# Attention probabilities of twelve heads turned by VectorE and a trip through device memory instead of by TensorE

## The chip, the cores and the metric

The kernel runs on one core of a Trainium2 chip. The metric is device time in microseconds for one execution. The core's engines work from separate instruction queues: TensorE (PE in the profile, its weight loads PEld), VectorE (DVE), ScalarE (ACT), GpSimd (POOL) and SyncE (SP), which here only issues transfers. An instruction that has to wait holds up whatever stands behind it in its own queue.

## The reference, cut to what matters

The program is a two-layer decoder trunk over 256 tokens of width 1024. Each layer is a half-weighted SwiGLU block of width 2816, a mixer, and a second SwiGLU block.

```python
for layer in range(2):
    h = h + 0.5 * swiglu(rms_norm(h, ffn1_norm[layer]), ...)
    hn = rms_norm(h, mix_norm[layer])
    h = h + (ab_mixer(hn, ...) if layer % 2 == 0 else c_mixer(hn, ...))
    h = h + 0.5 * swiglu(rms_norm(h, ffn2_norm[layer]), ...)
return rms_norm(h, final_norm)

def swiglu(x, w_gate, w_up, w_down):
    return (silu(x @ w_gate) * (x @ w_up)) @ w_down
```

The even layer's mixer (`ab_mixer`) has 8 attention heads of 64 with three dilated windows beside a gated position mixing; the odd layer's (`c_mixer`) has 16 heads of 64 with block-sparse attention. At 256 tokens both come down to causal softmax attention over all 256 keys, the even one with a mask that counts in how many windows a key lies. Per head this is

```python
p = softmax(q @ k.T * 64 ** -0.5 + mask)     # 256 queries x 256 keys, causal
out = p @ v
```

## The kernel before

**Numbers.** Every matrix is used as a high part (rounded to the matmul's format, float32r) and a low part (the rest). A product is three matmuls: high x high, high x low, low x high (`mm3`, L265). `split` (L270) makes both parts of a tile: ScalarE copies the high part, VectorE subtracts it for the low one.

**Weights.** They come as 171 pieces of up to 1 MB (`raw`) through SyncE's queue. `Stream` keeps three raw buffers (`RAW`) and four pairs of parts (`SPL`). `take` hands TensorE the next piece; `free` gives a piece back, and `pump` then splits the piece four ahead (L172 on ScalarE, L173 on VectorE) and issues the load three further on (L139).

**Order.** Inside the framework a planner puts each engine's instructions in a fixed order before the run, by its own estimate of when inputs are ready and by the order in which they are written. `tc.issue_after(x)` makes the instructions in its block stand behind `x` on the engine that both use. A tile's buffer is handed to the next tile of its name when everything that reads the old one is done; a transfer that reads it counts.

**Steps.** The mixers write the order of the attention work by hand. `Slots.at((5, 6, ...), f)` says at which step `f` is called; `step()` is called after every tile of matmuls, so step n comes right behind the n-th one. A step of the projections is 24 matmuls of 256 columns or 12 of 512. In the odd layer steps 0 to 3 are the first q and k tiles, 4 to 7 a block of v, 8 to 11 q and k of the second column group, 12 to 15 q and k of the third, 16 to 19 v, 20 to 23 q and k of the fourth, and 24 to 31 lie in the output projection. In the even layer 4 to 7 are v, 8 to 11 the gate's values, 12 to 19 u, q and k, and 20 to 27 the projection.

**Attention of a head.** `put_q` and `put_k` (L665, L677) make q and k with both parts from TensorE's banks; k's low half is written by GpSimd (L685) in the odd layer. `scores(h)` (L691) is four matmuls (L700, L701), then per half: VectorE adds the mask and takes the maximum (L704), ScalarE the exponential and its sum (L707), VectorE the reciprocal (L710), GpSimd (VectorE for the last heads) the multiplication (L714). The result is `pr`, 128 x 384: the first 128 queries with 128 keys, and the second 128 queries with 256. `turn(h)` (L718) transposes it on TensorE in three pieces of 128 x 128 (L723) into a bank and splits it into `pth` and `ptl` (L726). `weighted(p)` (L728) multiplies a pair of heads with v, three matmuls of 512 columns and three of 256, and splits the result into `mix`.

In the odd layer before, the heads' scores stand at steps 5 to 8, 12 to 19, 24, 24, 25 and 25; their turns at 9, 9, 11, 11, 16, 16, 18, 18, 20, 20, 22, 22, 26, 26, 27 and 27; the eight sums at 11, 13, 18, 20, 22, 24, 28 and 29. In the even layer scores stand at 6 to 9, 20, 20, 21, 21, turns at 10, 10, 12, 12, 22, 22, 23, 23, sums at 13, 14, 24, 25.

The kernel already has one trip through device memory: `turn_back` in the last SwiGLU block (L486) turns the residual in blocks of 32 x 32 on VectorE (L491, a 32 x 32 block stays in its place among the blocks), sends 512 KB to memory (`away`, L494) and fetches it with its blocks moved (`xr`, L496, four fetches of 128 KB).

Of the kernel before, what the change touches and what calls it, by code (L numbers as in the profile page):

```python
# [35 lines left out]
LINE, SHIFT = 64, 16  # L36
EDGE, GAP = 56, 240

# [76 lines left out]
class Stream:  # L115


    def __init__(self, nc, pools, weights):
        self.nc, (self.raw_pool, self.hi_pool, self.lo_pool) = nc, pools
        self.weights = weights  # L120
        self.specs, self.raws, self.parts = [], {}, {}
        self.loaded = self.split = self.done = self.next = 0
        self.held = False

    def add(self, nk, w, shift, cuts, reset):
# [4 lines left out]
    def load_one(self, between=lambda i: None):  # L130
        j = self.loaded
        nk, w, loads, *_ = self.specs[j]
        raw = self.raw_pool.tile([128, CH], F32, name="raw")
        n = nk * w // loads
        for i in range(loads):
            between(i)
            cs = slice(i * n, (i + 1) * n)
            src = self.weights[j, i * 128 * n : (i + 1) * 128 * n].rearrange("(p c) -> p c", p=128)
            self.nc.sync.dma_start(raw[:, cs], src)  # L139
        self.raws[j] = raw  # L140
        self.loaded += 1
# [5 lines left out]
    def split_parts(self):  # L147
# [19 lines left out]
        def split(a, r):  # L167
            n = r.free_size()
            hi, lo = his[:, a : a + n], los[:, a : a + n]
            if len(r.shape) == 3:  # L170
                hi, lo = (t.rearrange("p (k c) -> p k c", k=reset) for t in (hi, lo))
            nc.scalar.activation(hi, r, AF.Copy)  # L172
            nc.vector.tensor_sub(lo, r, hi.bitcast(F32))  # L173

# [50 lines left out]
def trunk(ctx: ExitStack, tc: tile.TileContext, a, out):  # L225
# [11 lines left out]
    def bank():  # L237
        return ps.tile([128, 512], F32, name="bank")
# [406 lines left out]
    def make_attention(mp, mask_cols, nheads, v, mix, rows=False):  # L645

        qs, ks, probs, pts = {}, {}, {}, {}
        pairs, flying = (4, 5) if rows else (2, 4)
        seconds = [mp.tile([128, 2 * S + LINE], F32R, name=f"ql{i}") for i in range(pairs)]
# [7 lines left out]
        def scaled(bk):  # L657
            t = mp.tile([128, S], F32, name="qk", bufs=3)
            nc.vector.tensor_mul(t, bk[:, :S], norm["row"])
            return t  # L660
# [30 lines left out]
        def scores(h):  # L691
            q, ql = qs.pop(h)
            k = ks.pop(h)
            sc = bank()
            pr = mp.tile([128, 384], F32, name="pr", bufs=flying)
            nm = wk.tile([128, 2], F32, name="nm")
# [19 lines left out]
            return power, share  # L716

        def turn(h):  # L718
            p, j = divmod(h, 2)
            pr = probs.pop(h)  # L720
            tp = bank()
            for i in range(3):
                nc.tensor.transpose(tp[:, i * 128 : (i + 1) * 128], pr[:, i * 128 : (i + 1) * 128], ident)  # L723
            if j == 0:
                pts[p] = [mp.tile([128, 2, 384], F32R, name=n, bufs=2) for n in ("pth", "ptl")]
            return split(pts[p][0][:, j, :], pts[p][1][:, j, :], tp[:, :384])  # L726

        def weighted(p):  # L728
            o = bank().rearrange("p (j c) -> p j c", j=2)
            pth, ptl = pts.pop(p)  # L730
            vs = slice(p * 128, (p + 1) * 128)
            mm3(o, v[0][:, 0, vs], v[1][:, 0, vs], pth[:, :, :256], ptl[:, :, :256], True, False)
            mm3(o[:, :, 128:], v[0][:, 1, vs], v[1][:, 1, vs], pth[:, :, 256:], ptl[:, :, 256:], False, True)
            for j in range(2):
                r = slice(j * 64, j * 64 + 64)
                done = split(mix[0][r, p], mix[1][r, p], o[r, j, :].rearrange("p (t c) -> p t c", t=NT))
            return done

        return put_q, put_k, scores, turn, weighted

# [83 lines left out]
    def ab_mixer(phase):  # L824
        with tc.tile_pool(name="mp", bufs=1) as mp:
# [3 lines left out]
            uT = mp.tile([128, 4, S], F32, name="uT")  # L829
            put_q, put_k, scores, turn, weighted = make_attention(mp, slice(0, 384), 8, v, mix)  # L830

# [63 lines left out]
    def c_mixer(phase):  # L895
        with tc.tile_pool(name="mp", bufs=1) as mp:
            mix = mix_tiles(mp)
            v = v_tiles(mp, D)
            put_q, put_k, scores, turn, weighted = make_attention(mp, slice(384, 768), 16, v, mix, True)
# [90 lines left out]
```

## Time and profile before

| what | value |
|---|---|
| median of three runs | 937.8 us (937.56 to 938.14) |
| the profiled execution | 937.0 us |
| its span, first to last instruction | 935.3 us |
| granted TensorE clock | 0.999 |
| TensorE busy | 927.7 us, 99% |
| VectorE, ScalarE, GpSimd busy | 612.1, 499.2, 83.0 us |
| even layer's attention in the span | about 206 to 269 us |
| odd layer's attention in the span | about 655 to 740 us |

Busy time of TensorE is modelled: a matmul's length in the profile includes its pipeline, and the next one starts long before the last one ends. What an instruction costs the stream is the distance from its start to the next start. For the other engines the length is the cost, apart from small overlaps. A timeline row has start, length, engine, line, operation and tiles, then how many were merged. A row of the groups has after the bar the busy time in all, the mean in ns, and the idle time before it.

### The profile page before, as it was taken

The numbers are of one execution on the slowest core, as the hardware profiler recorded it, in microseconds if no ns is written. First come the engines' busy times: TensorE is split into PE (matmuls) and PEld (weight loads), VectorE is DVE, ScalarE is ACT, GpSimd is POOL, SyncE is SP. The second block draws the span as 40 slices with busy tenths as digits, with TensorE's granted clock in tenths as the row PEclk, the third lists the DMA queues.
The fourth block names the chain that finished last, engine by engine and source line by source line (L and its number), as shares of the span: only waits on it lengthen the run. The fifth ranks groups of instructions, "written<-read, shape, count | busy, mean of one in ns | idle before, by whom it ended". The sixth has DMA issues, their size and how long they took to land.

```text
span 935.3 us, 18101 instructions
## 1 busy us (share of the span) xinstructions
PE 927.7 (99%) x7655; PEld 907.4 (97%) x7655; DVE 612.1 (65%) x892; ACT 499.2 (53%) x782; POOL 83.0 (9%) x114
## 2 busy tenths in 40 slices
PE   9999999999999999999999999999999999999997
PEld 9999999999999999999999999999999999999886
DVE  7866556676888666555756665567787786656543
ACT  7744444468667454444454544456786665445431
POOL 0000000034210000000000000002574000000000
PEclk9999999999999999999999999999999999999999
DMA  8755554665336555555555555556543377555521
GB/s 320 281 212 181 189 194 162 223 222 180 136 136 226 188 211 188 183 175 206 204 184 200 204 180 170 203 184 220 177 139 136 137 243 269 186 188 210 190 90 46
DMA packets 28305, 176.99 MB, mean 189 GB/s; under 512 B 3264, under 2 KB 4672, under 8 KB 9152
## 3 DMA queue, kind: packets, MB, share of 16 engines
q1 hardware_dynamic: 26928, 173.65, 52.5%
q10 hardware_dynamic: 1296, 2.18, 0.7%
q8 instruction: 60, 0.98, 0.4%
q14 instruction: 21, 0.17, 0.0%
HBM read 173.72 MB, written 2.10 MB: 188 GB/s over the span
## 4 chain that ended last, share of the span: by engine, by line
PE 98%; issue 1%; DMA 0%; ACT 0%; SPq 0%; DVE 0%; POOLq 0%; POOL 0%
PE bank L266 30%; PE bank L267 30%; PE bank L268 30%; PE bank L567 2%; PE bank L571 2%; PE bank L568 2%; PE bank L723 1%; PE bank L700 1%; PE bank L701 1%; DMA x<-in_x 0%; PE bank L343 0%; PE bank L859 0%; PE bank L361 0%; PE bank L455 0%; PE bank L456 0%
## 5 line engine op out<-in xcount | busy, mean ns | idle before, releaser
L172 ACT ACTIVATE whi<-raw 128x1024 fp32r<-128x1024 f32 (+3 forms) x352 | 330.5, 985 | 350.1 <-issue 282.9
L173 DVE TENSOR_TENSOR wlo<-raw,whi 128x1024 fp32r<-128x1024 f32 (+3 forms) x352 | 389.6, 1141 | 126.7 <-ACT whi L172 125.8
L266 PE MATMUL bank<-xTh,whi 128*128 128x256 f32 x1616 | 447.9, 277 | 0.0
L267 PE MATMUL bank<-xTl,whi 128*128 128x256 f32 x1616 | 446.7, 276 | 0.0
L268 PE MATMUL bank<-xTh,wlo 128*128 128x256 f32 x1616 | 446.6, 276 | 0.0
L267 PEld LDWEIGHTS bank<-xTl,whi 128*128 128x128 f32 x1616 | 303.5, 188 | 0.2
L266 PEld LDWEIGHTS bank<-xTh,whi 128*128 128x128 f32 x1616 | 303.5, 188 | 0.0
L268 PEld LDWEIGHTS bank<-xTh,wlo 128*128 128x128 f32 x1616 | 303.5, 188 | 0.0
L267 PE MATMUL bank<-hTl,whi 128*128 128x256 f32 x528 | 145.8, 276 | 0.0
L266 PE MATMUL bank<-hTh,whi 128*128 128x256 f32 x528 | 145.8, 276 | 0.0
L268 PE MATMUL bank<-hTh,wlo 128*128 128x256 f32 x528 | 145.8, 276 | 0.0
L266 PEld LDWEIGHTS bank<-hTh,whi 128*128 128x128 f32 x528 | 99.1, 188 | 0.0
L268 PEld LDWEIGHTS bank<-hTh,wlo 128*128 128x128 f32 x528 | 99.1, 188 | 0.0
L267 PEld LDWEIGHTS bank<-hTl,whi 128*128 128x128 f32 x528 | 99.1, 188 | 0.0
L506 DVE TENSOR_TENSOR hm<-gs,bank 128x512 f32<-128x512 f32 x44 | 30.1, 687 | 77.7 <-PE bank L268 77.3
L503 DVE TENSOR_TENSOR gs<-bank,row 128x512 f32<-128x512 f32 x44 | 30.0, 689 | 47.8 <-PE bank L268 47.8
L266 PE MATMUL bank<-mixh,whi 128*128 128x256 f32 x128 | 35.3, 281 | 0.0
L267 PE MATMUL bank<-mixl,whi 128*128 128x256 f32 x128 | 35.1, 277 | 0.0
L268 PE MATMUL bank<-mixh,wlo 128*128 128x256 f32 x128 | 35.0, 277 | 0.0
L714 POOL TENSOR_SCALAR pr<-pr,rl 128x128 f32<-128x128 f32 (+1 forms) x36 | 30.8, 870 | 25.2 <-DVE rl L710 14.1
L653 POOL MEMSET ql<- 64x256 f32 x12 | 3.7, 307 | 328.7 <-ACT whi L172 170.3
L567 PE MATMUL bank<-whi,hTh 128*128 128x512 f32 x80 | 31.1, 389 | 0.0
(134 smaller groups left out, 877.4 us busy)
## 6 DMA issues: line engine op xcount, KB each, us to landing
raw<-in_weights SPq DMA_DIRECT2D x149, 1024.0 KB, 4.9
raw<-in_weights SPq DMA_DIRECT2D x12, 768.0 KB, 4.4
raw<-in_weights SPq DMA_DIRECT2D x6, 512.0 KB, 6.5
x<-in_x SPq DMA_DIRECT2D x4, 264.0 KB, 4.0
raw<-in_weights SPq DMA_DIRECT2D x4, 256.0 KB, 4.3
away<-xn SPq DMA_DIRECT2D x2, 512.0 KB, 5.5
xr<-away SPq DMA_DIRECT2D x8, 128.0 KB, 5.7
fg<-in_final_norm ACTq DMA_DIRECT2D x1, 512.0 KB, 3.7
```

The costliest lines, as they stand in the source:

```text
L172: nc.scalar.activation(hi, r, AF.Copy)
L173: nc.vector.tensor_sub(lo, r, hi.bitcast(F32))
L266: nc.tensor.matmul(p, sh, mh, start=start, stop=False)
L267: nc.tensor.matmul(p, sh, ml, start=False, stop=False)
L268: nc.tensor.matmul(p, sl, mh, start=False, stop=stop)
L503: nc.vector.tensor_mul(g, both(pg), twice(norm["row"]))
L506: nc.vector.tensor_mul(hm, g, both(pu))
L567: nc.tensor.matmul(banks[t, h], sh, w[0][kw][:, cs], start=k == 0, stop=False)
L568: nc.tensor.matmul(banks[t, h], sh, w[1][kw][:, cs], start=False, stop=False)
L571: nc.tensor.matmul(banks[t, h], sl, w[0][kw][:, cs], start=False, stop=k == FT - 1)
L700: nc.tensor.matmul(sc[:, b * S : (b + 1) * S], q[:, bs], k, start=True, stop=False)
L714: share = engine.tensor_scalar(pr[:, cs], pr[:, cs], rl[:, b : b + 1], None, op0=ALU.mult)
```

## The change

Heads 0 to 3 of the even layer and 0 to 7 of the odd layer, in groups of four, no longer go through `turn`. Instead, two steps behind the scores (three for head 3 of the even layer), `tilt(h)` transposes the 32 x 32 blocks of `pr` in place among the blocks on VectorE, into a tile `turned` that holds four heads. `send(g)` writes this tile to device memory in four transfers, in pieces of 512 bytes; `fetch(g)` brings it back in four transfers with the blocks moved, in pieces of 2 KB, into what will be `ptl`. Both go through SyncE's queue, the fetch right behind the send, and the next weight load behind the fetch (`st.turn`). Five steps later `part(g)` makes the high part on ScalarE and the low part in place on VectorE, in two halves each, behind the last split of weights that was written before it. The other twelve heads are turned on TensorE as before.

`pth` and `ptl` now hold four heads, a block of 32 queries at a time with the four heads beside each other, and have one buffer where pairs had two; `weighted` and its split read and write that order. `pr` has three buffers where it had five (odd) and four (even); the scores of the later heads go into `turned` and, in the odd layer, partly into `pr`. `qk` has two buffers where it had three, and an unused gap tile before the activations shrinks from 240 to 112 words. Scores, turns and sums of the odd layer move to other steps.

```diff
-EDGE, GAP = 56, 240
+EDGE, GAP = 56, 112
@@ Stream.load_one
-            self.nc.sync.dma_start(raw[:, cs], src)
+            with self.turn.pop()() if self.turn else ExitStack():
+                self.nc.sync.dma_start(raw[:, cs], src)
@@ Stream.split_parts
-            nc.scalar.activation(hi, r, AF.Copy)
-            nc.vector.tensor_sub(lo, r, hi.bitcast(F32))
+            self.last = nc.scalar.activation(hi, r, AF.Copy), nc.vector.tensor_sub(lo, r, hi.bitcast(F32))
@@ make_attention
-        pairs, flying = (4, 5) if rows else (2, 4)
+        pairs = 4 if rows else 2
+        late = nheads // 2
...
-            t = mp.tile([128, S], F32, name="qk", bufs=3)
+            t = mp.tile([128, S], F32, name="qk", bufs=2)
@@ scores
-            pr = mp.tile([128, 384], F32, name="pr", bufs=flying)
+            if h < late or rows and 12 <= h < 15:
+                pr = mp.tile([128, 384], F32, name="pr", bufs=3)
+            else:
+                if h % 4 == 0 or h == 15:
+                    probs["turned"] = turned_tile()
+                pr = probs["turned"].rearrange("p m j h r -> p (m j h r)")[:, h % 4 * 384 : (h % 4 + 1) * 384]
...
-            nc.vector.reciprocal(rl, l)
+            probs["behind"] = nc.vector.reciprocal(rl, l)
@@ new
+        def turned_tile():
+            return mp.tile([128, 3, 4, 4, 32], F32, name="turned")
+
+        def tilt(h):
+            if h % 4 == 0:
+                probs["turned"] = turned_tile()
+            turned = probs["turned"]
+            behind = st.last[1] if h % 4 == 3 else probs["behind"]
+            with tc.issue_after(behind.ins):
+                nc.vector.transpose(turned[:, :, :, h % 4].rearrange("p m j r -> p (m j) r"),
+                                    probs.pop(h).rearrange("p (b c) -> p b c", c=32))
+
+        def send(g):
+            sent[g] = dram.tile([32, 12, 4, 128], F32, name=f"sent{nheads}{g}")
+            for i in range(4):
+                nc.sync.dma_start(sent[g][:, :, i],
+                                  probs["turned"][i * 32 : (i + 1) * 32].rearrange("c m j h r -> c (m j) (h r)"))
+
+        def fetch(g):
+            src = sent.pop(g).rearrange("c (m j) i f -> j c m (i f)", j=4)
+            pts[g] = parts = part_tiles()
+            for j in range(4):
+                back = nc.sync.dma_start(parts[1][j * 32 : (j + 1) * 32].bitcast(F32).rearrange("p (m i) h r -> p m (i h r)", m=3),
+                                         src[j])
+            st.turn.append(lambda: tc.issue_after(back.ins))
+
+        def part(g):
+            with tc.issue_after(st.last[0].ins), tc.issue_after(st.last[1].ins):
+                for q in range(2):
+                    hi, lo = (t[:, q * 6 : (q + 1) * 6] for t in pts[g])
+                    nc.scalar.activation(hi, lo.bitcast(F32), AF.Copy)
+                    nc.vector.tensor_sub(lo, lo.bitcast(F32), hi.bitcast(F32))
+
+        def part_tiles():
+            return [mp.tile([128, 12, 4, 32], F32R, name=n) for n in ("pth", "ptl")]
@@ turn
-                pts[p] = [mp.tile([128, 2, 384], F32R, name=n, bufs=2) for n in ("pth", "ptl")]
-            return split(pts[p][0][:, j, :], pts[p][1][:, j, :], tp[:, :384])
+                pts[g] = part_tiles()
+            return split(*(t[:, :, j] for t in pts[g]), tp[:, :384].rearrange("p (b r) -> p b r", r=32))
@@ weighted
-            mm3(o, v[0][:, 0, vs], v[1][:, 0, vs], pth[:, :, :256], ptl[:, :, :256], True, False)
-            mm3(o[:, :, 128:], v[0][:, 1, vs], v[1][:, 1, vs], pth[:, :, 256:], ptl[:, :, 256:], False, True)
+            for b, (q, n) in enumerate(((slice(0, 8), 0), (slice(8, 12), 256))):
+                mm3(o[:, n:], v[0][:, b, vs], v[1][:, b, vs],
+                    *(t[:, q, hs].rearrange("p b h r -> p b (h r)") for t in pts[p // 2]), b == 0, b == 1)
@@ ab_mixer
-            slots.at((10, 10, 12, 12, 22), turn)
+            slots.at((8, 9, 10, 12), tilt)
+            slots.at((12,), send)
+            slots.at((12,), fetch)
+            slots.at((17,), part)
+            slots.at((22,), lambda _: turn(4))
...
-            slots.at((13, 14, 24), weighted)
+            slots.at((18, 19, 24), weighted)
@@ c_mixer
-            slots.at((5, 6, 7, 8, 12, 13, 14, 15, 16, 17, 18, 19, 24, 24, 25, 25), scores)
-            slots.at((9, 9, 11, 11, 16, 16, 18, 18, 20, 20, 22, 22, 26, 26, 27, 27), turn)
-            slots.at((11, 13, 18, 20, 22, 24, 28, 29), weighted)
+            slots.at((5, 6, 7, 8, 11, 12, 13, 14, 17, 18, 19, 20, 23, 24, 25, 25), scores)
+            slots.at((7, 8, 9, 10, 13, 14, 15, 16), tilt)
+            slots.at((10, 16), send)
+            slots.at((10, 16), fetch)
+            slots.at((15, 21), part)
+            slots.at((16, 17, 22, 22, 25, 26, 28, 29), weighted)
+            slots.at((23, 23, 24, 24, 26, 26, 27, 27), lambda i: turn(8 + i))
```

More of the change, by code (lines that the diff above doesn't have):

```diff
@@ L123, in __init__ @@
         self.held = False
+        self.turn = []
     def add(self, nk, w, shift, cuts, reset):
@@ L724, in turn @@
             if j == 0:
-                pts[p] = [mp.tile([128, 2, 384], F32R, name=n, bufs=2) for n in ("pth", "ptl")]
-            return split(pts[p][0][:, j, :], pts[p][1][:, j, :], tp[:, :384])
+                pts[g] = part_tiles()
+            return split(*(t[:, :, j] for t in pts[g]), tp[:, :384].rearrange("p (b r) -> p b r", r=32))
         def weighted(p):
-            o = bank().rearrange("p (j c) -> p j c", j=2)
-            pth, ptl = pts.pop(p)
+            o = bank()
+            hs = slice(p % 2 * 2, p % 2 * 2 + 2)
             vs = slice(p * 128, (p + 1) * 128)
-            mm3(o, v[0][:, 0, vs], v[1][:, 0, vs], pth[:, :, :256], ptl[:, :, :256], True, False)
-            mm3(o[:, :, 128:], v[0][:, 1, vs], v[1][:, 1, vs], pth[:, :, 256:], ptl[:, :, 256:], False, True)
+            for b, (q, n) in enumerate(((slice(0, 8), 0), (slice(8, 12), 256))):
+                mm3(o[:, n:], v[0][:, b, vs], v[1][:, b, vs],
+                    *(t[:, q, hs].rearrange("p b h r -> p b (h r)") for t in pts[p // 2]), b == 0, b == 1)
             for j in range(2):
                 r = slice(j * 64, j * 64 + 64)
-                done = split(mix[0][r, p], mix[1][r, p], o[r, j, :].rearrange("p (t c) -> p t c", t=NT))
+                done = split(*(m[r, p].rearrange("p t (i r) -> p (t i) r", r=32) for m in mix),
+                             o[r].rearrange("p (b h r) -> p b h r", h=2, r=32)[:, :, j])
             return done
-        return put_q, put_k, scores, turn, weighted
+        return put_q, put_k, scores, tilt, send, fetch, part, turn, weighted
     def mix_tiles(mp):
@@ L829, in ab_mixer @@
             uT = mp.tile([128, 4, S], F32, name="uT")
-            put_q, put_k, scores, turn, weighted = make_attention(mp, slice(0, 384), 8, v, mix)
+            put_q, put_k, scores, tilt, send, fetch, part, turn, weighted = make_attention(mp, slice(0, 384), 8, v, mix)
             vgain = mp.tile([128, 512], F32, name="vgain")
```

6 lines of the change are left out of this document (3 added, 3 removed).

## The prediction

> **What bounds the kernel now.** I read the page's engine shares and its chain first, to see which engine sets the end.
>
> ```profile
> span 935.3 us, 18101 instructions
> ...
> PE 927.7 (99%) x7655; PEld 907.4 (97%) x7655; DVE 612.1 (65%) x892; ACT 499.2 (53%) x782; POOL 83.0 (9%) x114
> ...
> PE 98%; issue 1%; DMA 0%; ACT 0%; SPq 0%; DVE 0%; POOLq 0%; POOL 0%
> ...
> L723 PE MATMUL bank<-ident,pr 128*128 128x128 f32 x72 | 9.9, 273 | 0.0
> ```
>
> TensorE is busy from end to end and the chain is its own stream. So time taken out of that stream shortens the run one for one, and every wait put into it lengthens it one for one. The last row, from the groups by line, is what the change halves: 72 transposes, three for each of 24 heads. Its 273 ns is the length of one with its pipeline, not what it costs the stream. For that I read TensorE's timeline, where the cost is the distance between starts.
>
> ```profile
> 216.92 0.40 PE L266 MATMUL bank<-whi,xTh 128*128 128x512 f32 x1
> ...
> 219.68 0.82 PE L723 MATMUL bank<-ident,pr 128*128 128x128 f32 x6
> ...
> 223.09 0.28 PE L266 MATMUL bank<-xTh,whi 128*128 128x256 f32 x1
> ...
> 225.84 0.82 PE L723 MATMUL bank<-ident,pr 128*128 128x128 f32 x6
> ...
> 244.00 0.37 PE L266 MATMUL bank<-xTh,whi 128*128 128x256 f32 x1
> ...
> 665.38 0.28 PE L700 MATMUL bank<-k,q 128*128 128x256 f32 x1
> ...
> 665.84 0.28 PE L266 MATMUL bank<-xTh,whi 128*128 128x256 f32 x1
> ...
> 668.56 0.82 PE L723 MATMUL bank<-ident,pr 128*128 128x128 f32 x6
> ...
> 674.68 0.82 PE L723 MATMUL bank<-ident,pr 128*128 128x128 f32 x6
> ...
> 682.73 0.40 PE L266 MATMUL bank<-pth,vth 128*128 128x512 f32 x1
> ...
> 683.78 0.28 PE L266 MATMUL bank<-xTh,whi 128*128 128x256 f32 x1
> ...
> 690.14 0.40 PE L266 MATMUL bank<-whi,xTh 128*128 128x512 f32 x1
> ...
> 734.21 0.90 PE L723 MATMUL bank<-ident,pr 128*128 128x128 f32 x6
> ```
>
> From 216.92 to 219.68 run the twelve matmuls of one step of a token block, 2.76 us. From 219.68 to 223.09 run six transposes (two heads) and the same twelve again, 3.41 us: the six cost 0.65. In the odd layer one step of 24 small matmuls takes 2.72 us (665.84 to 668.56); six transposes and two such steps take 6.12 (668.56 to 674.68), which leaves 0.68. The stages also give the other steps: scores of a head 0.46 us (665.38 to 665.84), a weighted sum of a pair 1.05 (682.73 to 683.78).
>
> **What leaves TensorE.** Twelve heads (0 to 3 of the even layer, 0 to 7 of the odd one) lose their turns: six groups at 0.65 to 0.68 us, **4.0 us** off the path. Nothing is added to TensorE: scores and weighted sums keep their number. But all twelve pairs' sums now read the probabilities in runs of 64 words (eight or four runs a matmul), where before each matmul read two runs. Before, three matmuls at 512 and three at 256, with six gaps, take 1.05 us; the same sizes without a gap would be 3 x 2.76 / 12 + 3 x 2.72 / 24 = 1.03. I take zero; six gaps at 0.02 us make thirty gaps 0.10, which is 0.08 more a pair and bounds it at 1.0 us in all. The moved addresses (the smaller gap tile, the larger turned tile) I also take at zero: the three lines of the main matmuls read different tiles, and the page gives them 277, 276 and 276 ns.
>
> **What VectorE and ScalarE get.** These rows are from the groups by line with shapes apart.
>
> ```profile
> L173 DVE TENSOR_TENSOR wlo<-raw,whi 128x768 fp32r<-128x768 f32 x26 | 23.8, 954 | 26.1 <-ACT whi L172 25.8
> ...
> L173 DVE TENSOR_TENSOR wlo<-raw,whi 128x384 fp32r<-128x384 f32 x32 | 17.5, 576 | 5.0 <-ACT whi L172 5.0
> ...
> L271 DVE TENSOR_TENSOR ptl<-bank,pth 128x384 fp32r<-128x384 f32 x24 | 12.3, 547 | 2.1 <-ACT pth L271 2.0
> ...
> L491 DVE STREAM_TRANSPOSE xn<-x 128x128 f32<-128x128 f32 x16 | 3.6, 278 | 0.0
> ...
> L172 ACT ACTIVATE whi<-raw 128x768 fp32r<-128x768 f32 x26 | 20.7, 839 | 39.6 <-issue 39.6
> ...
> L271 ACT ACTIVATE pth<-bank 128x384 fp32r<-128x384 f32 x24 | 10.5, 486 | 0.5 <-PE bank L723 0.2
> ```
>
> For four heads VectorE loses four low parts at 547 ns (2.19 us) and gains four tilts and two low parts over 768 columns at 954 ns (1.91). A tilt of 384 columns lies between 576 ns (the plain operation of that width) and three times 278 (834); I take 0.58. That is +2.0 us a group, at most +3.1. ScalarE goes from four at 486 to two at 839, 0.3 less. Neither engine is the bound; what hides the extra is the lead of the weights' halves.
>
> ```profile
> 671.42 1.00 DVE L271 TENSOR_TENSOR ptl<-bank,pth 128x384 fp32r<-128x384 f32 x2
> ...
> 672.91 1.23 DVE L173 TENSOR_TENSOR wlo<-raw,whi 128x1024 fp32r<-128x1024 f32 x1
> 674.17 0.42 DVE L659 TENSOR_TENSOR qk<-bank,row 128x256 f32<-128x256 f32 x1
> ...
> 674.20 0.33 SPq L139 DMA_DIRECT2D raw<-in_weights  x1
> ...
> 690.49 1.05 ACT L172 ACTIVATE whi<-raw 128x1024 fp32r<-128x1024 f32 x1
> ...
> 675.13 1.54 POOL L685 TENSOR_TENSOR k<-qk,k 64x256 fp32r<-64x256 f32 x2 [2.46 <-ACT k L683]
> ...
> 225.92 1.49 DVE L173 TENSOR_TENSOR wlo<-raw,whi 128x1280 fp32r<-128x1280 f32 x1 [0.55 <-ACT whi L172]
> ...
> 690.00:710.00 20.00, 20.00 (x122) 17.74 (x121) 16.37 (x43) 16.64 (x43) 13.69 (x16) 1.00 0.38 138
> ```
>
> (Timelines of several engines, and last a stretch: VectorE is its fourth busy time, 16.37 of 20 us.) The chunk whose low half ends at 674.14 is four chunks ahead of TensorE, which takes it at 690.14: **16 us of cover** for VectorE and ScalarE. The load issued at 674.20 feeds the third split after it, at 690.49: also 16 us, of which a landing takes about 5. If that cover were gone, every late half would stall TensorE in full.
>
> **The queue of SyncE.** Each group adds four sends and four fetches of 197 KB to the queue that issues the weights. The fetches wait in it for the sends, and the next weight load stands behind them. The nearest rows are the existing trip through memory, in the queue's timeline and in the landings of its two lines (away, then back).
>
> ```profile
> 775.09 0.35 SPq L139 DMA_DIRECT2D raw<-in_weights  x1
> 775.49 0.43 SPq L494 DMA_DIRECT2D away<-xn  x1
> 779.93 0.33 SPq L139 DMA_DIRECT2D raw<-in_weights  x1
> 783.91 0.32 SPq L496 DMA_DIRECT2D xr<-away  x1
> ...
> DMA to landing us min/median/max: 2.6/5.5/8.4
> ...
> DMA to landing us min/median/max: 3.6/5.7/7.3
> ```
>
> A send behind a fresh load took 8.4 us (775.49 to 783.91), and ours also stands right behind one. Its pieces are 512 bytes instead of 4 KB, and there are 786 KB rather than 512. Nothing in the trace has that piece size. The quickest fetch (128 KB in 1 KB pieces) took 1.0 us longer than the quickest away (3.6 against 2.6), and three sends follow the first: I allow 0 to 3 us more, and take none, since 8.4 is already the longer of two. The last of four fetches is issued 3 x 0.43 = 1.3 us after the first and lands in 3.6 (nothing ahead of it) to 5.7. So the trip, call it T, is 5.5 + 1.3 + 3.6 = 10.4 at best, 8.4 + 3 + 1.3 + 5.7 = 18.4 at worst. I take 8.4 + 1.3 + 3.6 = **13.3**, because the queue holds no load while the fetches go. The weights are held up by T less a landing at most, about 8 us, under the 11 left of their cover: no cost.
>
> **Is the trip done in time?** After the landing the part needs 0.84 + 2 x 0.95 = 2.75 us, then the weighted sum can start.
>
> Odd layer, first group: step 9 ends at 668.56, and without turns step 10 ends at 671.3. The last tilt is queued behind the low half that ends at 674.14 now. It loses the 1.00 us of ptl ahead of it and gains a tilt, so the sends start at 673.2 to 674.7, say 673.95. TensorE reaches the weighted sum after six more steps and four scores: 671.3 + 6 x 2.72 + 4 x 0.46 = 689.5. Late by 673.95 + 13.3 + 2.75 - 689.5 = 0.5 us. Even layer: sends at 225.92 + 1.49 - 0.66 + 0.58 = 227.3, ready at 243.4; TensorE is there at 244.00 + 2.72 less two turns (1.3) and two sums (2.1) = 243.3. Late by 0.1. Odd layer, second group: its fetch must also wait for the first group's second sum, which ends at 694.8, but the sends (step 15 ends at 686.7; 5.6 us from a freed chunk to its low half, as from 668.56 to 674.14, and a tilt: 692.9) land at 701.3, later. Ready at 708.9, wanted at 709.8: 0.9 to spare.
>
> One more: the odd layer's head 4 is scored at step 11, one step after its k instead of two. Now k's chain from the bank's end (671.9, a step before 674.68) to the first of two POOL rows (675.13 + 0.77) is 4.0 us, with the two ptl and a half of weights ahead of it. Without ptl it is 3.0 against a step of 2.72, a wait of 0.3, which lies ahead of the first sum and so is part of the 0.5.
>
> **What else moves, at zero.** In the odd layer the turns of heads 8 to 11 and the sums of pairs 4 and 5 go from steps 20 to 24 into steps 23 to 26, beside the scores of heads 12 to 15. There stood the only turns that waited before, 0.90 instead of 0.82 (734.21). Steps 23 and 24 give VectorE two low parts each, but step 24 has one score less than before; the bound is a low part late for each of the two sums, 1.1 us. The smaller rings: pr (3) gets head 0 back at step 7, and head 3 is scored at step 8; qk (2) is read by GpSimd in 2 x 0.77 us, under a step. Head 4's tilt (step 13 ends at 680.8) overwrites what the first send reads until 682.4: VectorE can stand 1.6 us, inside the 16.
>
> **Sum.** 4.0 - 0.6 = **3.4 us less**. The profiled execution took 937.0 us, its span 935.3; the median of the three runs is 937.8, so I put the result at 937.8 - 3.4 = **934.4 us**, the profiled one near 933.6. Its own range is 933.4 (nothing late, 4.0, and 0.4 of scatter, where the three runs shown spread over 0.6) to 935.8 (the gapped reads and half of that last bound added).
>
> **Rivals.** *The trip is late: slower.* Place: the three weighted sums behind a part. With T each is late by T - 12.8, T - 13.3 and T - 14.2. At 14.0 they give back 1.9 us, at 14.8 all 4.0, at 16.0 they cost 7.7 and the kernel takes 941.5; at the 18.4 bound 15, 949. For it: 512-byte pieces, 1.5 times the bytes, 8.4 as the largest of two. Against it: 5.5 is their middle. It decides from T = 14.8. I give over 15.4 (slower by more than 0.2%) 0.22, and 14.0 to 15.4 (about 937, no change that shows) 0.14. Beside it stands a rule of the Trainium skill ("VectorE: DVE Perf Modes", section "Rules for kernel authors"): transpose 128x128 on TensorE where PSUM will do as destination, because VectorE only turns 32x32 blocks. It speaks against this change; no run here has yet shown the price of carrying the blocks around.
>
> *VectorE stands.* Heads 8 to 11 of the odd layer are scored into the turned tile that the second send still reads. Scores of head 8 come at 693.8, the send lands at 701.3: VectorE can stand 7.5 us, with low halves, the v evictions and the second part queued behind. It is 82% busy there, so by 709.8 it wins back 1.5; part of the remaining 6, less the 0.9 to spare, falls on the third weighted sum. Half of it, 2.5 us, gives 936.9. For it: the order is fixed before the run. Against it: the order is made by a planner that may put other work first. 0.11, spread over all three signs.
>
> *The transposes cost their full length.* 36 at the 273 ns of the first fence are 9.8 us and give 928.0. Against it: starts stand 0.1 us apart, and the 0.65 above includes the knock-on. 0.03. The Trainium skill ("TensorE: Matmul & The Clock Gate", Part 4: PE-mode transpose) gives about 275 ns for one in a kernel. The length agrees with the 273 here, but priced by it the gain would be 9.9 us, and the distances between starts say otherwise.
>
> **How the numbers follow.** 0.2% is 1.9 us, about what a measurement of this kernel can tell from no change: faster is under 935.9, slower over 939.7. Forecast 0.50; late trip 0.14 unchanged and 0.22 slower; VectorE stands 0.11 (0.03, 0.05, 0.03); full length 0.03. Faster 0.50 + 0.03 + 0.03 = 0.56, same 0.14 + 0.05 = 0.19, slower 0.22 + 0.03 = 0.25. The range goes from 933.0 to 942.0: it leaves out the full-length case and the late trips with T over 16.1, about 0.15 together.
>
> **What would show it.** Right: 36 transposes instead of 72; first fetch of a group issued under 9 us after its first send; no row of TensorE idle before a weighted sum by over 0.6 us. Wrong: sends that take over 10 us; the high part of a fetched group waiting on ScalarE for a DMA while TensorE waits at that sum; VectorE idle for a DMA ahead of head 8's scores; a wait for k ahead of head 4's; weight halves that end less than 5 us before their use.

## The result, and the profile after

The changed kernel takes 961.97 us (median of four runs, 960.96 to 966.56) against 937.68 for the kernel before on the same chip: a ratio of 1.027, 95% interval 1.0235 to 1.0301. The forecast was 934.4 with a range up to 942.0. The change is **24 us slower**. In this and the later runs some executions hold stretches of 20 to 400 us in which all matmuls start 3.8% further apart at a full granted clock (last section), which is why several ranges in brackets are wide; the ratios leave out executions more than 1.5% above the quickest.

The page of the changed kernel (an execution of 961.7 us), in the same parts as above: span, busy time, the chain by engine.

```profile
span 960.0 us, 18053 instructions
...
PE 931.5 (97%) x7619; PEld 908.4 (95%) x7619; DVE 616.7 (64%) x898; ACT 499.3 (52%) x776; POOL 83.9 (9%) x114
...
PE 88%; DVE 3%; ACT 3%; issue 2%; DMA 1%; POOL 1%; SPq 0%; POOLq 0%; ACTq 0%; DVEq 0%
```

TensorE has 36 instructions fewer, yet the chain that sets the end now runs over other engines for 12% of the span instead of 2%. That share is not TensorE's idle time, because the chain follows the work behind a wait back a long way; what TensorE itself waited is in the list of its waits (engine and line, what released it, us in all, times, longest).

```profile
PE bank L267 <- ACT pth L758: 17.6, 3, 7.8
PE bank L707 <- POOL k L687: 1.2, 1, 1.2
PE bank L908 <- DVE vn L902: 1.1, 1, 1.1
PE bank L443 <- DVE warm L436: 1.1, 1, 1.1
PE bank L456 <- ACT whi L174: 0.8, 1, 0.8
PE bank L268 <- DVE ptl L759: 0.4, 1, 0.4
```

The same list of the kernel before has one row.

```profile
PE bank L442 <- DVE warm L435: 1.1, 1, 1.1
```

Three weighted sums wait 17.6 us for the high part of a fetched group, 0.4 for a low part; head 4's scores wait 1.2 for k, and the first piece of the even layer's position mixing waits 1.1 for vn, its normalised input. TensorE's timeline and its stretches (mean granted clock is the PEclk column, behind five busy times) show what comes behind such a wait.

```profile
252.87 0.80 PE L267 MATMUL bank<-pth,vth 128*128 128x512 f32 x1 [7.62 <-ACT pth L758]
253.46 0.42 PE L267 MATMUL bank<-xTh,whi 128*128 128x256 f32 x1
253.68 0.41 PE L268 MATMUL bank<-xTl,whi 128*128 128x256 f32 x1
...
706.27 0.50 PE L267 MATMUL bank<-pth,vth 128*128 128x512 f32 x1 [2.24 <-ACT pth L758]
...
734.19 1.22 PE L267 MATMUL bank<-pth,vth 128*128 128x512 f32 x2 [7.75 <-ACT pth L758]
```

```profile
244.00:250.00 6.00, 1.25 (x12) 1.05 (x10) 5.29 (x12) 3.83 (x7) 3.67 (x5) 1.00 0.54 214
250.00:254.00 4.00, 1.13 (x4) 0.84 (x4) 3.00 (x5) 2.41 (x4) 0.58 (x1) 0.54 0.73 260
254.00:258.00 4.00, 4.00 (x21) 3.81 (x21) 0.84 (x2) 0.76 (x2) 0.00 (x0) 0.61 0.01 2
258.00:262.00 4.00, 4.00 (x35) 3.87 (x34) 1.26 (x3) 2.38 (x5) 0.00 (x0) 1.00 0.00 0
```

While TensorE stands, or 1.4 us after the short wait, its granted clock falls to a half, and it stays there when the work is back: two matmuls of 256 columns start 0.22 us apart (253.46 and 253.68) instead of 0.113, and the stretch from 254 to 258 holds 21 matmuls, the next one 35. The trace has the half clock from 250.3 for 6.83 us, from 707.7 for 3.41 and from 731.6 for 6.83. TensorE works in about 12 of these 17 us and does half as much, so they cost about 6.

**The balance.** The span is 24.7 us longer. Waits 17.6 + 0.4 + 1.2 + 1.1, clock 6, and 0.8 at the start that the kernel before didn't wait, less the 4.0 of the transposes, make 23.1; 1.6 are left. About 1 of it lies between 750 and 790 us, where matmuls of 256 columns start 116.6 ns apart instead of 113.3.

**Was the trip late?** SyncE's queue for the even layer and the odd layer's two groups (four transfers in each row), and the landings of sends and of fetches.

```profile
231.11 2.71 SPq L741 DMA_DIRECT2D sent<-turned  x4
236.25 2.51 SPq L749 DMA_DIRECT2D ptl<-sent  x4
...
684.36 3.18 SPq L741 DMA_DIRECT2D sent<-turned  x4
690.64 2.50 SPq L749 DMA_DIRECT2D ptl<-sent  x4
...
704.95 3.44 SPq L741 DMA_DIRECT2D sent<-turned  x4
714.01 2.50 SPq L749 DMA_DIRECT2D ptl<-sent  x4
...
DMA to landing us min/median/max: 2.8/4.2/4.9
...
DMA to landing us min/median/max: 3.2/3.9/4.9
```

The last fetch of a group is issued 1.9 us after the first and lands 4.3, 4.9 and 4.2 us later (the two landing lines are over all twelve): at 242.5, 697.5 and 720.1. From the first send that is T = 11.4, 13.1 and 15.1, the third one because its fetch had to wait for group 0's second sum. TensorE had its work ahead of the sums behind it, and came to them, at 245.1, 703.9 and 726.3. So **each group lay in memory on the chip 2.6 to 6.4 us before TensorE came to its sum**. Even with the 2.75 us of the part, two were in time and the first would have been late by 0.2 us at most. ScalarE's timeline tells where they lost it.

```profile
241.87 0.86 ACT L674 ACTIVATE q<-qk 64x256 fp32r<-64x256 f32 x2 [1.05 <-DVE qk L661]
243.85 0.42 ACT L916 ACTIVATE mixh<-tmp 128x256 fp32r<-128x256 f32 x1 [1.12 <-DVE tmp L914]
...
245.04 1.04 ACT L174 ACTIVATE whi<-raw 128x1024 fp32r<-128x1024 f32 x1
245.98 0.84 ACT L674 ACTIVATE q<-qk 64x256 fp32r<-64x256 f32 x2
246.84 1.06 ACT L174 ACTIVATE whi<-raw 128x1024 fp32r<-128x1024 f32 x1
248.90 0.42 ACT L916 ACTIVATE mixh<-tmp 128x256 fp32r<-128x256 f32 x1 [0.99 <-DVE tmp L914]
250.37 0.85 ACT L685 ACTIVATE k<-qk 64x256 fp32r<-64x256 f32 x2 [1.05 <-DVE qk L661]
251.24 1.58 ACT L758 ACTIVATE pth<-ptl 128x768 fp32r<-128x768 f32 x2
...
704.65 1.56 ACT L758 ACTIVATE pth<-ptl 128x768 fp32r<-128x768 f32 x2
...
732.56 1.58 ACT L758 ACTIVATE pth<-ptl 128x768 fp32r<-128x768 f32 x2
```

The first row ends at 242.7, when the even group has landed. Then ScalarE works through two weight halves, a q, three mixings (one is not shown) and a k of later steps, idling in between for VectorE, while TensorE stands from 245.1 on; the part is its next instruction only at 251.24, 8.7 us after its landing. Its order was fixed before the run. The other two parts start 7.2 and 12.5 us after theirs.

### The profile page after: what moved, and what is told of

The parts are those of the page before. It is cut to its first block, busy times and chain, and to the rows that moved or that the text cites. A ratio compares the mean times of both kernels' runs of the same rounds, so it can differ in the third digit from the quotient of the medians.

```text
span 960.0 us, 18053 instructions
## 1 busy us (share of the span) xinstructions
PE 931.5 (97%) x7619; PEld 908.4 (95%) x7619; DVE 616.7 (64%) x898; ACT 499.3 (52%) x776; POOL 83.9 (9%) x114
## 4 chain that ended last, share of the span: by engine, by line
PE 88%; DVE 3%; ACT 3%; issue 2%; DMA 1%; POOL 1%; SPq 0%; POOLq 0%; ACTq 0%; DVEq 0%
PE bank L268 27%; PE bank L267 27%; PE bank L269 27%; PE bank L569 2%; PE bank L572 2%; PE bank L568 2%; DVE wlo L174 2%; ACT whi L174 1%; DMA raw<-in_weights 1%; DMA x<-in_x 0%; ACT pr L714 0%; PE bank L770 0%; ACT pth L758 0%; PE bank L707 0%; POOL turned L721 0%
## 5 line engine op out<-in xcount | busy, mean ns | idle before, releaser
L569 PE MATMUL bank<-wlo,hTh 128*128 128x512 f32 x80 | 31.2, 390 | 0.0
```

The lines of the kernel that those rows point to most:

```text
L569: nc.tensor.matmul(banks[t, h], sh, w[1][kw][:, cs], start=False, stop=False)
```

## The experiments

All times are against the kernel before on the same chip; each ratio is with its 95% interval. The diffs are cut to what matters.

**The layout alone.** All twenty-four heads are turned by TensorE, into the new tiles. `pr` has its old number of buffers again, and the odd layer its old steps, but for two turns that stand one step later.

```diff
-            slots.at((8, 9, 10, 12), tilt)
-            slots.at((12,), send)
-            slots.at((12,), fetch)
-            slots.at((17,), part)
-            slots.at((22,), lambda _: turn(4))
+            slots.at((10, 10, 12, 12, 22), turn)
...
-            slots.at((18, 19, 24), weighted)
+            slots.at((13, 14, 24), weighted)
```

> All sixteen plus eight heads are still turned by TensorE, but into the change's tile of four heads (columns split in blocks of 32), read with gaps by the weighted sums and put in place by two-level addresses; two heads are turned one step later. It prices what the prediction set at nothing. Theory (the layout costs nothing): 937.7 us, within 0.5. Rival (gapped reads slow the 72 sums' matmuls by the 14 ns bound, or the turned tile's single buffer holds the sums): 938.7 or more, with starts of L268 and L269 further apart than 113 ns in the sums.

938.65 us (937.96 to 939.31), ratio 1.0011 (1.0003 to 1.0020). Its only new wait inside the mixers is `PE bank L702 <- DVE k L687: 1.2, 1, 1.2` in the list of waits: k of the even layer, not a gapped read.

**The same with three buffers of qk** (`bufs=2` to `bufs=3` at L660).

> The run with the layout alone, with three buffers for qk as in the kernel before, where the change has two. Theory (the 0.9 us of the layout are a wait of 1.4 us of head 4's scores at 252.7, since k's scaling stood 1.6 us later on VectorE for want of a buffer, and gapped reads cost nothing): 937.4 to 938.0. Rival (gapped reads or two-level addresses): 938.5 as before.

937.88 (936.98 to 941.57), ratio 1.0009 (1.0000 to 1.0018). The wait for k is gone from the list, so the smaller qk ring made it. In time the two runs can't be told apart. The gapped reads show in TensorE's timeline of this run:

```profile
683.24 0.40 PE L267 MATMUL bank<-pth,vth 128*128 128x512 f32 x1
...
684.28 0.28 PE L267 MATMUL bank<-xTh,whi 128*128 128x256 f32 x1
```

A pair's sum with gaps takes 1.04 us of the stream, against 1.05 in the kernel before (682.73 to 683.78 in the prediction's rows), so the gaps cost nothing that shows. For gapped reads and addresses together, the medians leave 0.5 us, the interval at most 1.7.

**Without the way through memory.** The parts are made straight from the tilted tile; this leaves out the second half of the transpose.

```diff
-                    nc.scalar.activation(hi, lo.bitcast(F32), AF.Copy)
-                    nc.vector.tensor_sub(lo, lo.bitcast(F32), hi.bitcast(F32))
+                    t = sent[g, 0].rearrange("p m j h r -> p (m j) h r")[:, q * 6 : (q + 1) * 6]
+                    nc.scalar.activation(hi, t, AF.Copy)
+                    nc.vector.tensor_sub(lo, t, hi.bitcast(F32))
...
-            slots.at((10, 16), send)
-            slots.at((10, 16), fetch)
-            slots.at((15, 21), part)
+            slots.at((11,), part)
+            slots.at((17,), lambda _: (weighted(1), part(1)))
```

> The change without its way through memory: nothing is sent or fetched, and the parts are taken straight from the tilted tile (the pieces of 32 rows are then not in their places, so this leaves out the second half of the transpose). It keeps the tilts, the parts, the layout, and 36 transposes instead of 72. Theory (the loss is in when the parts come, not in the work that was added to VectorE and ScalarE): the three waits of 7.9, 2.6 and 8.0 us are gone and the clock stays up, so 937.7 - 4.0 + at most 1.3 for head 4's k and 1.3 for the mixing's wait: 933.7 to 936.3. Rival (tilts and parts themselves hold up VectorE and so TensorE): 945 or more, with waits of TensorE on DVE above 3 us in all.

941.43 (940.47 to 944.91), ratio 1.0048 (1.0034 to 1.0061). The waits for parts are gone and the clock stays at 1.00, but the result lies between the two expectations: 3.7 us above the kernel before, not 1.4 to 4 under it. The waits that are left, above 0.5 us and without the one at the start:

```profile
PE bank L707 <- POOL k L687: 2.9, 2, 1.7
...
PE bank L910 <- DVE vn L904: 0.9, 1, 0.9
PE bank L707 <- DVE mixl L272: 0.9, 2, 0.7
PE bank L772 <- POOL turned L721: 0.6, 1, 0.6
```

None is for a part of a tilted group. They are the steps around it.

**Without tilts and parts too.** The sums of the changed groups read a constant; this leaves out their probabilities.

```diff
+                for t in parts:
+                    nc.gpsimd.memset(t.rearrange("p b h r -> p (b h r)").bitcast(F32), 0.5)
...
-            slots.at((7, 8, 9, 10, 13, 14, 15, 16), tilt)
```

> The run without the way through memory, and without the tilts and the parts as well: the weighted sums of the three changed groups read a constant tile (this leaves out these heads' probabilities). TensorE's order of work is that of the change, VectorE and ScalarE have less to do than in the kernel before. Theory (what the run without the way through memory lost, 941.4 against 933.7, is TensorE waiting for VectorE and ScalarE behind the tilts and parts): 933.5 to 935.5. Rival (TensorE, sooner by its missing transposes, only meets sooner what VectorE, ScalarE and GpSimd always had to do): the waits for the mixing's vn (1.2 us) and for head 4's k (1.3 us) stay, 936 to 939.

940.51 (936.73 to 953.78), ratio 1.0026 (0.9995 to 1.0057). Four of its twelve executions took 936.7 to 937.2, the rival's figure, three 940.2 to 940.5 and five 947.8 and more; the page is of one of 950.3. On it vn (1.1 us), k (0.7) and a turned head (0.6) are still waited for with nothing added to VectorE. So by the four quickest executions 0.5 to 1 of the 4.0 us that leave TensorE arrives at the end; the interval alone would not show a gain. Of the rest, 2.4 us are these waits for work that stood just in time before.

**The trip with nobody reading it.** As without the trip, but sends and fetches go, into a place in memory (`unread`).

```diff
-            pts[g] = parts = part_tiles()
+            unread = dram.tile([128, 3, 512], F32, name=f"unread{nheads}{g}")
...
-                back = nc.sync.dma_start(parts[1][j * 32 : (j + 1) * 32].bitcast(F32).rearrange("p (m i) h r -> p m (i h r)", m=3),
-                                         src[j])
+                back = nc.sync.dma_start(unread[j * 32 : (j + 1) * 32], src[j])
```

> As the run without the way through memory, but with the twelve sends and twelve fetches on SyncE, at the change's steps and ahead of the weights' loads; the fetched data goes to a place that nobody reads. It prices the traffic and the held queue alone. Theory (weights have cover): within 0.5 us of the run without it. Rival (held loads or crowded DMA engines make weights late): 3 us or more over it, with TensorE waiting for splits whose raw tile came late.

946.78 (945.56 to 947.58), ratio 1.0095 (1.0082 to 1.0108): 5.4 us over the run without, the rival's number. But TensorE waits for no weight. It waits 4.5 us in all for turned heads, `PE bank L771 <- POOL turned L721: 4.5, 4, 3.1`, and VectorE's and SyncE's timelines show why.

```profile
704.75 2.42 SPq L749 DMA_DIRECT2D unread<-sent  x4
...
720.45 0.34 DVE L711 CUSTOM_DVE_ANT_0 turned<-bank,mask,score 128x128 f32<-128x128 f32 x1
```

The fetch at 704.75 can go because the sends are done, and the second part, which reads the tile in this run, ends at 703.9, so the tile is free then. Yet VectorE scores head 8 into it only at 720.45, behind 15 us of other work; without the trip the same instruction stands at 705.09. The planner had laid it further back. That it did so because it took the send to be slow is an inference; the next run tests whether the tile is what held it.

**The same, with heads 8 to 10 in tiles of their own.**

```diff
-            if h < late or rows and 12 <= h < 15:
+            own = 11 if rows else 4
+            if h < late or rows and h in (8, 9, 10, 15):
                 pr = mp.tile([128, 384], F32, name="pr", bufs=3)
             else:
-                if h % 4 == 0 or h == 15:
+                if h == own:
                     probs["turned"] = turned_tile()
```

> The run whose fetched data nobody reads, with heads 8 to 10 in tiles of their own, so that their scores don't need the tile that group 1 sends. Theory (the 5.4 us over the run without the way through memory are scores laid behind the send of that tile): the wait of 3.9 us for the turned heads goes, 941 to 943.5. Rival (they are the traffic itself, held weights' loads or crowded engines): 946 to 947.5 as before.

941.06 (939.58 to 956.87), ratio 1.0032 (1.0015 to 1.0049), level with the run without any trip (1.0034 to 1.0061). So **twelve sends and twelve fetches cost nothing that shows by their traffic**, within about 2 us; the 5.4 us were a place in an order.

**The whole change, parts early in the queues.** What is traced in the next steps stands behind the part (`part` at step 16, released at 19; odd layer 14 and 20, released at 20 and 25).

```diff
+            behind[g] = ExitStack()
+            for b in parted:
+                behind[g].enter_context(tc.issue_after(b.ins))
```

> The whole change, but each group's parts stand earlier in ScalarE's and VectorE's queues: what is written in the next three to six steps is issued behind them. Theory (place in the queue): the waits before the sums fall from 7.9 to about 1.5 us, from 2.6 to at most 1, from 8.0 to about 4.5, and with them some of the 2.3 us per wait that the halved clock takes: 946 to 953 us. Rival (the way through memory takes that long): the waits end with the fetches, 960 to 963 us as before.

947.99 (942.91 to 950.61), ratio 1.0098 (1.0074 to 1.0121), in the theory's range. The page is of an execution that took 942.9. ScalarE's timeline and the waits:

```profile
244.93 1.56 ACT L758 ACTIVATE pth<-ptl 128x768 fp32r<-128x768 f32 x2
```

```profile
PE bank L267 <- ACT pth L758: 3.4, 2, 2.0
PE bank L707 <- POOL k L687: 1.4, 1, 1.4
PE bank L916 <- DVE vn L910: 1.1, 1, 1.1
```

The same trip, with nothing changed in it: the first part starts at 244.93 instead of 251.24, and the waits for high parts fall from 17.6 to 3.4 us (1.0 for low ones). The loss was the parts' place.

**The change with its sums two steps later**, parts as they were.

```diff
-            slots.at((16, 17, 22, 22, 25, 26, 28, 29), weighted)
-            slots.at((23, 23, 24, 24, 26, 26, 27, 27), lambda i: turn(8 + i))
+            slots.at((18, 19, 24, 24, 26, 26, 28, 29), weighted)
+            slots.at((25, 25, 25, 25, 26, 26, 27, 27), lambda i: turn(8 + i))
```

> The change with the weighted sums of the three groups two steps later, nothing else done for the parts. Theory (the sums come too early for parts whose place ScalarE's queue sets): a step is about 2.8 us of TensorE, so waits of 7.9, 2.6 and 8.0 us fall by up to 5.5 each, with the halved clock of the long ones: 943 to 951 us. Rival (the parts move back with TensorE, since what stands ahead of them in ScalarE's queue waits for TensorE): 957 to 962.

948.39 (948.03 to 950.23), ratio 1.0119 (1.0101 to 1.0136), inside the theory's range. The waits for high parts are 3.9 us, for low ones 1.8. Both ways to bring part and sum into order win 14 us by the medians.

**Parts early, own tiles, and head 4's scores one step later** (`11` to `12` in the odd layer's scores; the odd layer's first part at step 15).

> The run with the parts earlier in their queues, with heads 8 to 10 in tiles of their own and head 4's scores one step later, behind its k. Theory: head 4's wait (1.4 us) goes and group 1's parts no longer stand behind the exps of heads 8 to 11, which were behind the send: 948.0 becomes 941 to 945. Rival (the fetch, which waits for the sums of group 0, sets group 1's parts): only head 4's wait goes, 946 to 947.

944.59 (943.54 to 950.66), ratio 1.0087 (1.0061 to 1.0113), in the theory's range; but the profile has the wait for parts at 4.1 us, longest 2.7, now with the third part waiting for its fetch.

**Everything mended at once**, and the same without the early parts. Own tiles and head 4's step are as in the run above; the sums stand later (even layer 19, 20; odd layer 17, 18, 24, 24), the mixings at 16, 16, 17, 17.

> The whole change with everything that the runs point to: parts early in their queues, heads 8 to 10 in tiles of their own, head 4's scores and the mixings one step later, the sums of the first two groups one step later and those of the third two steps. Theory: the waits at 233 (1.4), 245 (2.3), 695 (1.2) and 713 us (3.8) go, some 8 us from 943.5: 935 to 938. Rival (no room on VectorE and ScalarE): 940 or more.

> As the run with everything, but the parts where the change has them in their queues. Theory (parts stand 6 to 9 us late there, and one step of the sums buys 2.8 us): 5 to 10 us over that run, 941 to 948. Rival (with the sums later, the parts' place no longer matters): within 1 us of it.

949.68 (948.99 to 950.59), ratio 1.0132 (1.0118 to 1.0147), and 956.13 (951.74 to 956.38), ratio 1.0188 (1.0172 to 1.0204). The difference of 6.5 us has the size that the theory gave, but not its cause: on the second page matmuls of 256 columns start 117.5 ns apart from 710 to 890 us, on the first 113.5 from 740 to 890, and that makes about 6 us. What the pair does show is the waits for high parts, 10.8 us without the early parts and no row in the list with them. The full set itself came out 11.7 us above its theory's range. Its waits:

```profile
PE bank L708 <- POOL k L687: 7.5, 1, 7.5
PE bank L267 <- DVE mixl L272: 2.0, 1, 2.0
```

The parts' waits are nearly gone, and TensorE waits for k of a later step instead: ahead of its scaling ScalarE and VectorE now do a part and weight halves.

**Mended places without the trip**, and **without tilts and parts** (mixings and head 4 one step later; own tiles in the first).

> The run without the way through memory with three places mended: heads 8 to 10 in tiles of their own, head 4's scores in the second mixer one step later, the first and the third mixing one step later. It is to show whether any order banks the missing transposes. Theory (the 7 us are waits of single steps that come too early by 1 to 2 us): waits at 233, 675 and 717 go, 5 us less: 935.5 to 937. Rival (VectorE and ScalarE have no room left in these stretches, a wait that goes comes back later): 939.5 to 941.5.

> The run without the way through memory, tilts and parts (the sums of the changed groups read a constant tile), with the first and third mixing and head 4's scores one step later. Theory (36 transposes are 3.5 us of TensorE, and only steps that came too early kept them from the end): 934 to 935 in its undisturbed executions. Rival (a wait mended comes back at the next step): 936.5 to 938.

944.08 (940.77 to 946.07), ratio 1.0067 (1.0050 to 1.0085), and 940.08 (935.96 to 953.83), ratio 1.0021 (0.9997 to 1.0045). In the first the rival's mechanism shows: the wait for vn goes, and TensorE waits 1.6 and 2.4 us for k instead. Its time lies above both ranges, and its page (946.1 us) has starts 117.8 ns apart from 770 to 880 us, so the time says little. In the second the five quickest of twelve executions are 935.96 to 936.76, about 1.0 under the kernel before, between the two expectations; vn is gone, and 2.2 us of waits stand at the even layer's later scores and turns.

**The full set with only the first mixer's sums later**, and **the odd layer's group 1's sums too**.

> The whole change with parts early, heads 8 to 10 in tiles of their own, head 4's scores and the mixings one step later, and only the sums of the first mixer one step later. Theory (each wait is mended at its place): the waits at 233 (1.4) and 245 us (2.3) go from the 943.5 of the run without these two, the 1.2 and 3.8 us of the second mixer stay: 939.5 to 941. Rival (they come back at the next step): 943 to 945.

> As the run before it, with the sums of the second mixer's group 1 two steps later as well. Theory: the wait of 3.8 us at 713 goes too: 936 to 938, at or under the kernel before. Rival (the place of these sums shifts k and the scores on VectorE and ScalarE, as in the run with all sums later): 944 or more.

941.09 (939.59 to 946.43), ratio 1.0047 (1.0029 to 1.0065): at the top of the theory's range, and the quickest form of the whole change that was run. One long wait is left, 2.5 us for the third part, which waits 1.1 us for its fetch and starts right behind the landing. Putting that sum two steps later gave 946.06 (945.52 to 946.57), ratio 1.0092 (1.0079 to 1.0105), with k waiting 7.5 us, as the rival said. **No form of the change was found that beats the kernel before.**

## Why the prediction was wrong

**The step that failed** is the sentence "After the landing the part needs 0.84 + 2 x 0.95 = 2.75 us, then the weighted sum can start". The durations held: 834 and 955 ns. But the part does not start at the landing. It starts at its place in ScalarE's fixed order, 8.7, 7.2 and 12.5 us later, and TensorE waits 17.6 us for it. The prediction looked at what the part would have to wait for, and at cover for what stands behind it; it never asked what the planner puts ahead of it. Its rival *VectorE stands* says that the planner sets the order, but used that as an argument for the change. Two ways to close the gap between part and sum, in the queues or on TensorE, each won 14 of the 24 us. Of the signs of being wrong that it gave, the wait for k came; the high part waited, too, but for its turn and not for a DMA.

**A term that was not there.** A wait of 7.6 us costs about 10, since the halved clock outlasts it. The three waits cost 6 us more by this.

Step by step:

- *Transposes, 4.0 us off:* held as far as the balance can tell. That nearly all of it reaches the end did not. TensorE is the bound, but it was not alone: with tilts and parts left out, the quickest executions gained 0.5 to 1 us.
- *Gapped reads and addresses, zero:* held for the gaps (1.04 against 1.05 us a sum); the addresses were not run alone. *The smaller qk ring, zero:* 1.2 us of wait in the run of the layout alone.
- *Tilt 0.58 us:* 555 ns over twelve in the groups by line. VectorE's busy time went from 612.1 to 616.7.
- *T = 13.3:* 11.4, 13.1, 15.1. The term was 1.9 us too long for the first group and right for the second, and the even group's sends left at 231.11, not at 227.3. The odd layer's first scores stood 9.8 us later than before, behind the even layer's loss. The third T came from the fetch behind group 0's sum, which the prediction had named and thought hidden.
- *Head 4's k, 0.3:* 1.2. k's scaling was late on VectorE; GpSimd began at 684.34, right behind ScalarE's k.
- *Mixing's vn:* not foreseen, 1.1. Without four turns TensorE comes to it sooner; the same 1.1 us stands in the run without tilts and parts.
- *Held loads, no cost:* held within about 2 us (the unread trip with own tiles).
- *Late trip* was the rival with the right place, the three sums behind a part, and at its bound nearly the right waits (15 us, 17.6 measured). Its cause was wrong, so that likeness is luck: no T of the first two groups reached its 14.8, and the third, 15.1, landed 6.2 us before its sum. *VectorE stands* named the right tile; the price, 5.4 us in the unread trip, came from the order and not from standing. *Full length of the transposes* fell with the sign.
- The rule of the Trainium skill ("VectorE: DVE Perf Modes", section "Rules for kernel authors") that keeps 128 x 128 transposes on TensorE came out right for this kernel, though not by the price of moving the blocks of 32: the traffic of the trip cost nothing that shows, and the part behind it waited in a queue.

Open: a form in which the third group's part comes in time without a late k (in the quickest form its fetch, held by group 0's second sum, sets it); where the rest of the 4.0 us goes beyond the 2.4 us of waits; and 0.6 us of the balance.

## What to carry to other kernels

Where a planner fixes each engine's order, a consumer behind a transfer starts at its place in its queue, not at the landing. Before costing the transfer, list what stands ahead of that consumer and whether the planner's idea of the transfer is slower than the chip's; then set the consumer's place and the place of what uses its result together.

An engine at 99% is the bound, but its neighbours may run just in time: freeing 4 us of it gave at most 1. Price what it meets sooner.

## What the runs showed of the hardware

**Idle time and the clock.** Over all traces, single idle stretches of TensorE up to 1.7 us left the granted clock at 1.00. Of eight from 1.9 to 2.7 us six were followed by 3.41 us at a half (among them 1.96, 1.97 and 2.70; one of 1.99 had a second of 1.77 right behind it), two were not (1.94 and 2.44). With waits of 3.1 to 7.8 us came 6.83 us at a half, partly within the wait, and with one of 10.3 came 10.24: multiples of 3.41. The Trainium skill ("TensorE: Matmul & The Clock Gate", section "Part 1: The HAM clock gate") gives about 3.4 us of idleness for it; here shorter waits did it too.

**Slower matmuls at full granted clock.** The same stretch of the SwiGLU blocks, in the kernel before and in the run without tilts and parts:

```profile
300.00:400.00 100.00, 100.00 (x885) 100.00 (x884) 62.04 (x66) 47.67 (x58) 0.00 (x0) 1.00 0.54 192
```

```profile
300.00:400.00 100.00, 100.00 (x851) 100.00 (x851) 60.89 (x66) 46.59 (x58) 0.00 (x0) 1.00 0.53 186
```

885 matmuls against 851, with the clock column at 1.00 in both: those of 256 columns start 117.6 ns apart instead of 113.3, 3.8% more. On that page this lasts from about 250 to 660 us. What brings it is open.
